# Inverse square roots as one power on POOL, and a column product as a pair of products, in a two-layer hybrid block

## The chip, the cores and the metric

The kernel runs on one core of a Trainium2 chip. The metric is the device time of one execution in microseconds. The names of the engines are those of the profile: PE is the matrix engine (PEld its weight loads), DVE the vector engine, ACT the scalar engine, POOL the GpSimd engine, SP the engine that issues the transfers.

## The reference

Two layers over 1024 latent and 256 context tokens of width 1024. Each layer normalises and modulates its input, projects it once, and runs three mixers side by side: a state space scan in two directions, grouped-query attention, and differential attention. Their outputs are concatenated and projected. What matters here are the places where a root mean square is inverted:

```python
def rmsnorm(x, g):
    xf = x.astype(jnp.float32)
    y = xf * lax.rsqrt(jnp.mean(xf * xf, axis=-1, keepdims=True) + EPS)
    return y.astype(x.dtype) * g
...
        # scan: one root per token
        return rmsnorm(y * jax.nn.silu(z.astype(y.dtype)), norm_g).astype(z.dtype)
...
        # grouped-query attention: one root per token and head, 4 query and 2 key heads
        q = rmsnorm(p["gq"].reshape(bb, ll, GQA_HEADS, GQA_HEAD_DIM), q_g)
        k = rmsnorm(p["gk"].reshape(bb, ll, GQA_KV_HEADS, GQA_HEAD_DIM), k_g)
...
        # differential attention: two maps, combined, then one root per token and head
        o = attention(q[:, :, 0::2], k[:, :, 0::2], v) - lam * attention(q[:, :, 1::2], k[:, :, 1::2], v)
        o = (rmsnorm(o, norm_g) * (1.0 - lam_init)).astype(v.dtype)
```

The layer's own norms, before the input projection and behind the output projection, are of the same form over 1024 columns.

## The kernel before, in words

Tokens lie in 10 tiles of 128 (two of context, eight latent). A layer runs through stages that overlap at their borders: the split of the input, the projections with the convolution, the scan (a chunk of each direction a step) beside the projections in token rows, the two attentions with the output projection in their gaps, and the layer's end. In the first layer the scan and the token rows lie from about 390 to 640 us of the profile and the attention from there to about 1060; in the second layer the attention lies from about 1620 to 2050.

The program is written engine by engine with few explicit orders: a scheduler takes the instructions with their priorities and fixes each engine's order when the program is built, and each engine then works through its list in that order. So an instruction that waits holds everything behind it on its engine.

The change concerns these helpers, by the names of tiles that the profile shows:

- `rsqrt` makes x to the power -0.5 from the exponent's guess (`nri`, `nrj`: L114, L116) and three Newton steps of three instructions each (`nrt`, `nrt`, `nrr`: L121 to L123), all on DVE: eleven instructions on a tile of 128 rows and 1 to 6 columns.
- `finish` (L732) ends a chunk of the scan: gate, the sum of squares `sa` by ACT, mean and eps on DVE (L741), the root, the product (`yf`, L743) and four transposes on PE.
- `gqa_norm` (L892) normalises the heads of a token tile: ACT squares, DVE sums to `gss` (L899), mean and eps on DVE (L900), the root, the product (`raw`, L902), then the rotation on DVE and POOL.
- `out_b` (L1331) ends an attention head: for the differential kind POOL squares (`osq`), DVE sums to `dss` (L1353), mean and eps on DVE (L1354), the root, and POOL multiplies (`oo`, L1356, and `yk`, L1359).
- `inv_rms` (L221) makes a layer norm's root; its mean and eps (`oms`, L223) read PSUM and stay on DVE.
- `s_pair` (L1279) combines the two maps' exponentials of a row: the first 1024 columns by one DVE instruction (L1292), the last 256 on POOL by a product with a column `cc` (L1296) and a sum (L1297).

POOL's main work in the attention is `pl` (L129), the trailing part of the transposed weights, for which PE's second pass of P V (L1416) waits.

Of the kernel before, what the change touches and what calls it, by code (L numbers as in the profile page):

```python
# [8 lines left out]
F32 = mybir.dt.float32  # L9
# [10 lines left out]
KT = 8            # contraction tiles of the model width  # L20
NT = 10           # token tiles: 0, 1 context, 2..9 latent
# [4 lines left out]
# columns of the per-layer parameter pack  # L26
# [41 lines left out]
def block_kernel(ctx: ExitStack, tc: tile.TileContext, tok, cvec, wmod, pack,  # L68
# [7 lines left out]
    @contextmanager  # L76
    def shifted(by):
        """instructions that the scheduler takes for earlier ones by so many."""
        tc.cur_priority -= by
        yield  # L80
        tc.cur_priority += by
# [13 lines left out]
    pm = []                            # the pack's part that the modulation needs  # L95
# [13 lines left out]

    def rsqrt(x, shape, tag, pl=None):  # L110
        """x -> x**-0.5 elementwise, from the exponent's guess and three Newton steps."""
        pl = pl or small
        yi = pl.tile(shape, I32, name="nri", tag=f"nri{tag}")
        V.tensor_scalar(yi, x.bitcast(I32), 1, None, op0=ALU.logical_shift_right)  # L114
        yj = pl.tile(shape, I32, name="nrj", tag=f"nrj{tag}")
        V.tensor_scalar(yj, yi, -1.0, float(0x5F3759DF), op0=ALU.mult, op1=ALU.add)  # L116
        y = yj.bitcast(F32)
        t = pl.tile(shape, F32, name="nrt", tag=f"nrt{tag}")
        r = pl.tile(shape, F32, name="nrr", tag=f"nrr{tag}")
        for i in range(3):  # L120
            V.tensor_mul(t, y, y)  # L121
            V.scalar_tensor_tensor(t, t, -0.5, x, op0=ALU.mult, op1=ALU.mult)
            V.scalar_tensor_tensor(r, t, 1.5, y, op0=ALU.add, op1=ALU.mult)  # L123
            y = r
        return r

    def lo_part(eng, out_, full, hi):
        """out_ = full - hi, the rest of a value whose leading bits are in hi."""
        eng.tensor_tensor(out_, full, hi.bitcast(F32), op=ALU.subtract)  # L129
# [4 lines left out]
    # silu of the conditioning vectors: [p, k, (lat, ctx)]  # L134
    cth = cp.tile([P, KT, 2], F32, name="cth")
    s2 = cp.tile([P, KT, 32], F32, name="s2")          # a column group of the array wide
# [5 lines left out]
    # modulation of each layer, [p, k, (lat, ctx)]: shift, scale (with the pre-norm gain),  # L142
    # gate (with the post-norm gain)
# [4 lines left out]
    def mod_mm(ps, w, k, g):  # L148
        """a part of the modulation in column group g of the array, its rows 32 g and 32 g + 1."""
        TE.matmul(ps[32 * g:32 * g + 32], s2[:, k], w, start=k == 0, stop=k == KT - 1, tile_position=(0, 32 * g))  # L150

    def modulation(parts, mp, pp, tag):
        """two of (layer, 0: shift, 1: scale, 2: gate), a half of each in a column group of the
        array; a generator of small portions."""
# [34 lines left out]
    rnext = cp.tile([P, NT], F32, name="rnext")     # the next layer's 1 / rms of each token  # L189
    BLK = ((256, 512), (0, 256), (768, 512))        # latent tiles 2..5, context, tiles 6..9  # L190

    def broadcast_row(ps, r, n):
        """r [P tokens, n tiles] as rows on all partitions, [P, n * 128] in PSUM."""
        for j in range(n):
            TE.matmul(ps[:, cs(j)], r[:, j:j + 1].to_broadcast([P, P]), ident, start=True, stop=True)
# [3 lines left out]
    def split_input(name):  # L199
        """leading and trailing part of a layer's input, a tile per column tile."""  # L200
        pl = us.enter_context(pool(name, side="right"))
        return [pl.tile([P, 2, T], F32R, name=f"u{k}") for k in range(KT)]

    def u_tile(l, k, c0, n, hr, x, eng):
        """a tile of the modulated input, split, from the normalised one."""
# [7 lines left out]
    def stats(acc, n, pp, tag, bufs=2):  # L213
        """1 / rms per token from the squares' sums over the column tiles, [P tokens, n / 128]."""
# [11 lines left out]
    def column_squares(pl, ps, x, j):  # L226
        """adds the sums over column tile j's rows of the squares of x to the rows of a column group."""
# [5 lines left out]
    def column_stats(pl, ps, pp, tag):  # L233
        """1 / rms per token of those sums, of which each column group has 32 copies."""
# [14 lines left out]
    def square_sum(pl, acc, x, n, j):  # L249
        """sums of squares over the column tiles, the even and the odd ones."""  # L250
# [8 lines left out]
    u = split_input("u0")  # L259
    def start():  # L260
# [20 lines left out]
        def normalise(bi):  # L281
            """tokens' tiles of a block times 1 / rms, in place."""
# [9 lines left out]
        def mod_tile(q):  # L292
            """scale and shift of two column tiles."""
# [53 lines left out]
    def make_finish(l, ylast, wlast, d_op, hsrc):  # L347
        """the end of a layer: its last block's output, and the next layer's input.  A generator;
        the first portion ends when the next layer's input has its block 0."""
# [51 lines left out]
        def finish():  # L401
            with pool("ow", 2, space=PSUM) as pw, pool("tail", 2) as un:
# [7 lines left out]
                def chain():  # L410
                    """the chain of block 2, in an order of its own before what else there is."""
# [18 lines left out]
    for l in range(DEPTH):  # L430
# [3 lines left out]
        t0 = 2 if last else 0          # first token tile that has an output  # L434
# [13 lines left out]
        d_y = dp.tile([8, NT, P, 2, P], F32R, name=f"y{l}")       # leading and trailing parts  # L448
# [13 lines left out]
        # small per-layer values  # L462
        hw = lt_([P, 48], "hw")      # half of the conv's taps and bias
# [22 lines left out]
        NC1 = 4 if l else 3            # conv tiles that begin with the first blocks  # L486
# [6 lines left out]
        def dt_part(tp):  # L493
# [26 lines left out]
            V.tensor_mul(e_, e_, d_)            # s = e / (2 + e), log1p(e) = 2 atanh(s)  # L520
# [33 lines left out]
        def t_weights(wp, i):  # L554
            """columns tile i of the projection's weights, split."""
# [17 lines left out]
        def t_block(i, bi, w):  # L573
            """columns tile i of the projection, transposed, of a block of tokens."""
# [54 lines left out]
        # the first half; after the first layer block 2 comes later than the others  # L629
# [29 lines left out]
        with pool("wT", 4) as wp, pool("convr", 2) as rw2, pool("conv", 2) as vp:  # L659
# [11 lines left out]
            # the second half; beside it the output projection's weights are split, for later  # L671
# [34 lines left out]
        def state_step(c, dr, xb, S, first):  # L706
            """the state after chunk c (in direction dr) from the one before it."""
# [15 lines left out]
        def y_off(c, dr, bc, S):  # L723
            """what the state before chunk c gives to its outputs."""
# [7 lines left out]
        def finish(c, fp, nb=2):  # L732
            """gate, norm, transpose."""
# [7 lines left out]
            V.tensor_scalar(sa, sa, 1.0 / 512, 4 * EPS, op0=ALU.mult, op1=ALU.add)  # L741
            rr = rsqrt(sa, [P, 1], "s")
# [84 lines left out]
        def qk_split(ck, r, nh, d, nq=0):  # L827
            """r [P, nh * d] -> leading and trailing parts, the first nq heads scaled by DSCALE."""
# [22 lines left out]
        def store_twice(dst, src):  # L851
            """both halves of dst's rows from src [r, 4, 128]."""
# [4 lines left out]
        def dq_out(ck, sf, b0, t):  # L857
            """[qh; qh; ql; ql] of each map."""
# [6 lines left out]
        def dk_out(ck, sf, b0, t):  # L865
            """[kh; kl; kh; kl] of each map."""
# [4 lines left out]
        def gq_out(ck, sf, t, trp):  # L871
            """[qh; qh], [ql; ql]."""
# [4 lines left out]
        def rope(ck, raw, nh, hd, ctab, s_lo, s_hi, full):  # L877
            """raw [P, nh*2*hd] rotated in place by the tables ([P, hd] each, or [P, 2, hd])."""
# [13 lines left out]
        def gqa_norm(ck, raw, parts, t):  # L892
            """per-head norm and rotation of raw [P, heads * 64] in place; parts: (gain, first, heads)."""
# [6 lines left out]
            V.tensor_scalar(ss, ss, 1.0 / 64, EPS, op0=ALU.mult, op1=ALU.add)  # L900
            rr = rsqrt(ss, [P, nh], f"g{nh}")
# [10 lines left out]
        with pool("rot") as rp, pool("tokc", 2) as ck:  # L912
# [7 lines left out]
            gain = {}                                  # q gain with the scores' scale, k gain  # L920
# [4 lines left out]
            # rotary tables with the gains folded in  # L925
# [12 lines left out]
            # chunks: z | dq dk | gq gk gv | dv | gg dg  # L938
# [3 lines left out]
            def tok_chunk(ck, ch, first):  # L942
# [11 lines left out]
                for t in range(first, NT):  # L954
# [9 lines left out]
                    if ch in (0, 4):                   # twice the silu  # L964
# [73 lines left out]
        def load_head(kind, m, ph):  # L1038
            """the transposed leading / trailing parts, doubled, of a head's q and k."""
# [21 lines left out]
        def make_job(kind, m, tq, nq):  # L1061
# [8 lines left out]
            # score pairs: (row, map) twice  # L1070
# [18 lines left out]
        def prefetch(kind, n):  # L1089
            """loads of the head of a kind that comes next in the score rows, after job n."""  # L1090
# [6 lines left out]
        # halves of jobs in order: those of two jobs of different kinds take turns  # L1097
# [25 lines left out]
        # Per job (a head's queries of one block of token tiles): score rows (key axis free) with  # L1123
        # their maximum and exponential, then per key tile a transpose, the split and P V.
        # A differential head's two maps are combined before the transpose.  The score rows run
        # ahead of the key tiles' steps.
# [10 lines left out]
        def out_part(bi, k0, pp, tag, kept=None):  # L1137
            """mix columns k0 .. k0 + 3 of the output projection of a block, added to what is in d_op;
# [487 lines left out]
```

## Time and profile before

| what | value |
|---|---|
| runs | 2101.39 us median of 3 (2097.04 to 2106.61) |
| profiled execution | span 2095.2 us from its first to its last instruction |
| runs above that span | 1.8 to 11.4 us, by the median 6.2 us |
| mean granted TensorE clock | 0.935 |
| instructions | 31014 |

The time of the profiled execution around its span isn't given apart; the runs stand above the span by what the third line says. A busy share is a mean over stages that have different limits.

### The profile page before, as it was taken

The numbers are of one execution on the slowest core, as the hardware profiler recorded it, in microseconds if no ns is written. First come the engines' busy times: TensorE is split into PE (matmuls) and PEld (weight loads), VectorE is DVE, ScalarE is ACT, GpSimd is POOL, SyncE is SP. The second block draws the span as 40 slices with busy tenths as digits, with TensorE's granted clock in tenths as the row PEclk, the third lists the DMA queues.
The fourth block names the chain that finished last, engine by engine and source line by source line (L and its number), as shares of the span: only waits on it lengthen the run. The fifth ranks groups of instructions, "written<-read, shape, count | busy, mean of one in ns | idle before, by whom it ended". The sixth has DMA issues, their size and how long they took to land.

```text
span 2095.2 us, 31014 instructions
## 1 busy us (share of the span) xinstructions
PE 1822.2 (87%) x9936; PEld 1475.8 (70%) x9936; DVE 1565.1 (75%) x4103; ACT 1041.9 (50%) x1955; POOL 1162.7 (55%) x1007
## 2 busy tenths in 40 slices
PE   5899999898979999888988797998798898989885
PEld 4587777777767668777765486877777776768773
DVE  5777567777759878799858477577687787888974
ACT  4444233334347766676634354233333676767651
POOL 4535355654227657668735335556543577877741
PEclk9899999899989999999989898998998999999997
DMA  9157557856795988586665148668656956457455
GB/s 289 44 197 235 174 178 205 265 176 203 213 267 167 283 257 261 165 248 201 216 218 186 33 151 283 207 188 247 218 157 208 278 172 180 140 157 212 145 183 184
DMA packets 360003, 418.61 MB, mean 200 GB/s; under 512 B 38752, under 2 KB 252832, under 8 KB 359840
## 3 DMA queue, kind: packets, MB, share of 16 engines
q1 hardware_dynamic: 359840, 416.64, 64.0%
q8 instruction: 78, 1.28, 0.2%
q14 instruction: 85, 0.70, 0.1%
HBM read 282.18 MB, written 134.38 MB: 199 GB/s over the span
## 4 chain that ended last, share of the span: by engine, by line
PE 38%; DVE 26%; DMA 16%; POOL 6%; issue 6%; ACT 4%; SPq 3%; DVEq 0%; POOLq 0%; ACTq 0%
DVE pt L1244 6%; PE sc L1242 4%; DMA ab<-acs 3%; PE tp L1373 3%; PE prj L962 3%; PE prj L961 3%; PE prj L963 3%; PE ops L343 2%; PE ops L344 2%; PE ops L345 2%; PE po L1416 2%; PE po L1415 2%; DMA op<-o 2%; DMA q<-dq 2%; DMA wof<-in_wout_dram 2%
## 5 line engine op out<-in xcount | busy, mean ns | idle before, releaser
L129 POOL TENSOR_TENSOR pl<-pf,ph 128x512 fp32r<-128x512 f32 x283 | 374.2, 1327 | 197.2 <-DVE ph L1395 80.4
L1244 DVE TENSOR_SCALAR_CACHE_REDUCE pt<-sc 128x512 f32<-128x512 f32 (+1 forms) x600 | 335.3, 587 | 71.6 <-PE sc L1242 62.8
L1257 ACT ACTIVATE pt<-pt,nm 128x1280 f32<-128x1280 f32 x192 | 262.4, 1366 | 132.1 <-DVE nm L1255 130.1
L961 PE MATMUL prj<-wh,u 128*128 128x512 f32 (+1 forms) x768 | 298.8, 391 | 27.1 <-DVE th L967 13.7
L962 PE MATMUL prj<-wl,u 128*128 128x512 f32 (+1 forms) x768 | 295.9, 386 | 8.0 <-POOL wl L129 5.3
L963 PE MATMUL prj<-wh,u 128*128 128x512 f32 (+1 forms) x768 | 293.9, 384 | 0.0
L1373 PE MATMUL tp<-ident,pt 128*128 128x128 f32 x1312 | 209.5, 283 | 4.9 <-ACT pf L1383 3.5
L1416 PE MATMUL po<-pl,vt 128*128 128x256 f32 x644 | 184.4, 308 | 18.6 <-POOL pl L129 14.9
L1415 PE MATMUL po<-ph,vt 128*128 128x256 f32 x644 | 187.7, 304 | 14.5 <-ACT ot L1420 6.3
L1383 ACT COPY pf<-tp 128x512 f32<-128x512 f32 x289 | 166.6, 580 | 66.3 <-PE tp L1373 30.9
L961 PEld LDWEIGHTS prj<-wh,u 128*128 128x128 f32 x768 | 153.1, 200 | 54.3 <-DVE th L967 15.6
L1373 PEld LDWEIGHTS tp<-ident,pt 128*128 128x128 f32 x1312 | 160.4, 145 | 29.5 <-ACT pf L1383 8.2
L962 PEld LDWEIGHTS prj<-wl,u 128*128 128x128 f32 x768 | 153.6, 200 | 33.5 <-POOL wl L129 6.6
L1242 PE MATMUL sc<-dk,q 128*128 128x512 f32 (+1 forms) x400 | 148.2, 416 | 31.2 <-DVE pt L1244 21.3
L963 PEld LDWEIGHTS prj<-wh,u 128*128 128x128 f32 x768 | 153.6, 200 | 23.2
L1416 PEld LDWEIGHTS po<-pl,vt 128*128 128x128 f32 x644 | 126.8, 197 | 39.4 <-POOL pl L129 27.4
L1415 PEld LDWEIGHTS po<-ph,vt 128*128 128x128 f32 x644 | 127.1, 197 | 29.5 <-ACT ot L1420 9.5
L607 DVE SCALAR_TENSOR_TENSOR cacc<-craw,hw,cacc 128x1284 f32<-128x1284 f32 (+1 forms) x64 | 118.5, 1853 | 33.4 <-ACT cacc L604 21.9
L582 PE MATMUL prj<-u,wTh 128*128 128x512 f32 x256 | 108.4, 423 | 23.4 <-DVE u L210 17.0
L343 PE MATMUL ops<-y,wo 128*128 128x512 f32 (+1 forms) x304 | 119.0, 391 | 7.4 <-DMA y<-y 6.8
L1296 POOL TENSOR_SCALAR pt<-pt,cc 128x256 f32<-128x256 f32 x64 | 103.1, 1612 | 38.1 <-DVE cc L1288 16.1
L1242 PE MATMUL sc<-gk,q 128*128 128x256 f32 (+1 forms) x400 | 111.7, 384 | 14.1 <-DVE pt L1244 11.8
(287 smaller groups left out, 4448.1 us busy)
## 6 DMA issues: line engine op xcount, KB each, us to landing
wo<-wo SPq DMA_DIRECT2D x80, 512.0 KB, 4.8
wm<-in_wmod_dram SPq DMA_DIRECT2D x48, 512.0 KB, 5.9
dk<-dk SPq DMA_DIRECT2D x16, 1280.0 KB, 7.9
ab<-acs SPq DMA_DIRECT2D x18, 1024.0 KB, 7.6
wo<-wos SPq DMA_DIRECT2D x32, 512.0 KB, 3.6
wf<-in_wtok_dram SPq DMA_DIRECT2D x64, 256.0 KB, 4.0
y<-y SPq DMA_DIRECT2D x30, 512.0 KB, 5.5
op<-o SPq DMA_DIRECT2D x48, 256.0 KB, 4.4
```

The lines of the kernel that those rows point to most:

```text
L129: eng.tensor_tensor(out_, full, hi.bitcast(F32), op=ALU.subtract)
L343: TE.matmul(o, wa[:, k], y[:, :, 0], start=first, stop=False)
L961: TE.matmul(ps[:, c0:], uh, wh[k][:, c0:], start=k == 0, stop=False)
L962: TE.matmul(ps[:, c0:], uh, wl[k][:, c0:], start=False, stop=False)
L963: TE.matmul(ps[:, c0:], ul, wh[k][:, c0:], start=False, stop=k == KT - 1)
L1242: TE.matmul(ps[:, 0:b - a].rearrange("p (t c) -> p t c", c=P), q[:, jb.q0 + j], kt[:, a // P:b // P], start=x == 0, stop=x == len(qq) - 1)
L1244: V.tensor_scalar(ts[r][:, a:b], ps[:, 0:b - a], -1.0, None, op0=ALU.mult, op1=ALU.min, accum_out=mts[r][:, i:i + 1])
L1257: S_.activation(e, e, AF.Exp, bias=nm, scale=-1.0, accum_out=jb.s2[:, j, mp_:mp_ + 1])
L1373: TE.transpose(tp[:, j * P:(j + 1) * P], jb.pt[2 * hf + j % 2][:, cs(2 * s + j // 2)], ident)
L1383: S_.copy(pf[:, :w_], tp[:, :w_])
L1415: TE.matmul(o, vv, a[:, c], start=k == 0, stop=False)
L1416: TE.matmul(o, vv, b[:, c], start=False, stop=k == jb.nk - 1)
```

## The change

Each root becomes one instruction on POOL, a power with the tile `mhalf` of -0.5. For `finish`, `gqa_norm` and `out_b` the mean and eps go to POOL too (`inv_root`, tile `irm`). In `s_pair` the product with the column becomes a pair of products, the second with 1.0. The rest of the diff removes comments, so that line numbers move by one to four.

```diff
+    mhalf = cp.tile([P, 8], F32, name="mhalf")
+    G.memset(mhalf, -0.5)
+
     def rsqrt(x, shape, tag, pl=None):
         pl = pl or small
-        yi = pl.tile(shape, I32, name="nri", tag=f"nri{tag}")
-        V.tensor_scalar(yi, x.bitcast(I32), 1, None, op0=ALU.logical_shift_right)
-        yj = pl.tile(shape, I32, name="nrj", tag=f"nrj{tag}")
-        V.tensor_scalar(yj, yi, -1.0, float(0x5F3759DF), op0=ALU.mult, op1=ALU.add)
-        y = yj.bitcast(F32)
-        t = pl.tile(shape, F32, name="nrt", tag=f"nrt{tag}")
         r = pl.tile(shape, F32, name="nrr", tag=f"nrr{tag}")
-        for i in range(3):
-            V.tensor_mul(t, y, y)
-            V.scalar_tensor_tensor(t, t, -0.5, x, op0=ALU.mult, op1=ALU.mult)
-            V.scalar_tensor_tensor(r, t, 1.5, y, op0=ALU.add, op1=ALU.mult)
-            y = r
+        G.tensor_tensor(r, x, mhalf[:, 0:shape[1]], op=ALU.pow)
         return r
 
+    def inv_root(total, shape, mean, eps, tag):
+        m = small.tile(shape, F32, name="irm", tag=f"irm{tag}")
+        G.tensor_scalar(m, total, mean, eps, op0=ALU.mult, op1=ALU.add)
+        return rsqrt(m, shape, tag)
...
         def finish(c, fp, nb=2):
-            V.tensor_scalar(sa, sa, 1.0 / 512, 4 * EPS, op0=ALU.mult, op1=ALU.add)
-            rr = rsqrt(sa, [P, 1], "s")
+            rr = inv_root(sa, [P, 1], 1.0 / 512, 4 * EPS, "s")
...
         def gqa_norm(ck, raw, parts, t):
-            V.tensor_scalar(ss, ss, 1.0 / 64, EPS, op0=ALU.mult, op1=ALU.add)
-            rr = rsqrt(ss, [P, nh], f"g{nh}")
+            rr = inv_root(ss, [P, nh], 1.0 / 64, EPS, f"g{nh}")
...
             def s_pair(jb, pair):
-                        G.tensor_scalar(b, b, c[:, 1:2], None, op0=ALU.mult)
+                        G.tensor_scalar(b, b, c[:, 1:2], 1.0, op0=ALU.mult, op1=ALU.mult)
...
             def out_b(jb):
-                    V.tensor_scalar(ss[:, :nq], ss[:, :nq], 1.0 / 64, EPS, op0=ALU.mult, op1=ALU.add)
-                    rr = rsqrt(ss[:, :nq], [P, nq], f"a{nq}")
+                    rr = inv_root(ss[:, :nq], [P, nq], 1.0 / 64, EPS, f"a{nq}")
```

The program has 69 roots: 18 in `finish` (one column), 20 in `gqa_norm` (18 of six columns, 2 of two), 20 in `out_b` (16 of four, 4 of two) and 11 in `inv_rms` (four or two). All but those of `inv_rms` move their mean and eps too, 58 instructions. The order of every engine is made anew by the scheduler, so that it differs in many places. Two of them matter here.

On DVE, in `gqa_norm` of the first layer's fourth token tile, the order before is this, from the sum of squares to the first product of the second Newton step (a second and third step of the same three instructions follow, and then `raw<-raw,nrr`):

```order
L899 TENSOR_REDUCE gss<-gsq 128x6
L900 TENSOR_SCALAR gss<-gss 128x6
L114 TENSOR_SCALAR nri<-gss 128x6
L116 TENSOR_SCALAR nrj<-nri 128x6
L121 TENSOR_TENSOR nrt<-nrj 128x6
L122 SCALAR_TENSOR_TENSOR nrt<-nrt,gss 128x6
L123 SCALAR_TENSOR_TENSOR nrr<-nrt,nrj 128x6
L121 TENSOR_TENSOR nrt<-nrr 128x6
```

And this is DVE's order at the same place of the changed kernel:

```order
L897 TENSOR_REDUCE gss<-gsq 128x6
L899 TENSOR_TENSOR raw<-raw,nrr 128x384
L879 TENSOR_TENSOR t_4253<-raw,Sqg 128x4x32
L881 TENSOR_TENSOR t_4253<-raw,Sqg 128x4x32
L879 TENSOR_TENSOR t_4258<-raw,Skg 128x2x32
```

The product that needs the root now stands right behind the sum, with nothing of DVE's between the two.

POOL's order at that tile before is this:

```order
L890 TENSOR_TENSOR raw<-raw,t_4270 128x256
L129 TENSOR_TENSOR vs<-raw,vs 128x2x64
L890 TENSOR_TENSOR raw<-raw,t_4275 128x128
L129 TENSOR_TENSOR st<-raw,st 128x6x64
L129 TENSOR_TENSOR vs<-raw,vs 128x2x64
```

In the changed kernel it is this:

```order
L123 TENSOR_SCALAR irm<-gss 128x6
L117 TENSOR_TENSOR nrr<-irm,mhalf 128x6
L128 TENSOR_TENSOR st<-raw,st 128x6x64
L128 TENSOR_TENSOR vs<-raw,vs 128x2x64
L888 TENSOR_TENSOR raw<-raw,t_4253 128x256
```

The mean and the power stand ahead of the split `st` of the tile before and of this tile's `vs`, so both now wait for DVE's sum.

In the attention, on POOL, this is the first layer's head of four blocks before, from the square's neighbour to the head's end:

```order
L1347 TENSOR_TENSOR yk<-oo,gg 128x2x64
L129 TENSOR_TENSOR pl<-pf,ph 128x512
L1296 TENSOR_SCALAR pt<-pt,cc 128x256
L1297 TENSOR_TENSOR pt<-pt 128x256
L129 TENSOR_TENSOR pl<-pf,ph 128x512 x2
L1356 TENSOR_TENSOR oo<-oo,nrr 128x256
L1359 TENSOR_TENSOR yk<-oo,gg 128x4x64
```

And this is the changed kernel at that head:

```order
L128 TENSOR_TENSOR pl<-pf,ph 128x512
L123 TENSOR_SCALAR irm<-dss 128x4
L1293 TENSOR_SCALAR pt<-pt,cc 128x256
L117 TENSOR_TENSOR nrr<-irm,mhalf 128x4
L1344 TENSOR_TENSOR yk<-oo,gg 128x2x64
L1294 TENSOR_TENSOR pt<-pt 128x256
L128 TENSOR_TENSOR pl<-pf,ph 128x512
L1352 TENSOR_TENSOR oo<-oo,nrr 128x256
```

The head's mean and power now stand among POOL's other work, ahead of a `pl` for which PE waits; the product of the maps' columns moved in between them.

## Rows read from the trace of the kernel before

**Rows 1.** The page: busy time of each engine, and the last chain's shares.
```profile
PE 1822.2 (87%) x9936; PEld 1475.8 (70%) x9936; DVE 1565.1 (75%) x4103; ACT 1041.9 (50%) x1955; POOL 1162.7 (55%) x1007
PE 38%; DVE 26%; DMA 16%; POOL 6%; issue 6%; ACT 4%; SPq 3%; DVEq 0%; POOLq 0%; ACTq 0%
```

**Rows 2.** Windows: length, busy PE, PEld, DVE, ACT, POOL, granted clock, DMA share.
```profile
700.00:850.00 150.00, 144.30 (x919) 109.05 (x918) 119.30 (x392) 101.16 (x194) 97.49 (x93) 1.00 0.86 265
850.00:1000.00 150.00, 127.72 (x762) 107.82 (x760) 133.60 (x423) 99.26 (x174) 110.90 (x96) 0.92 0.67 205
...
1480.00:1600.00 120.00, 101.50 (x512) 84.50 (x511) 97.35 (x337) 45.27 (x110) 56.67 (x58) 0.90 0.60 182
...
1700.00:1850.00 150.00, 132.26 (x801) 109.00 (x800) 125.90 (x409) 107.31 (x184) 115.30 (x95) 0.99 0.57 169
```

**Rows 3.** Whole-span sums of L114, L116, L121, L122, L123, L741, L900, L1354.
```profile
sum 2096.00, DVE 24.30; mean DVE 2.21
sum 2096.00, DVE 18.28; mean DVE 1.66
sum 2096.00, DVE 54.84; mean DVE 4.99
sum 2096.00, DVE 53.73; mean DVE 4.88
sum 2096.00, DVE 59.48; mean DVE 5.41
sum 2096.00, DVE 2.67; mean DVE 0.24
sum 2096.00, DVE 12.77; mean DVE 1.16
sum 2096.00, DVE 9.13; mean DVE 0.83
```

**Rows 4.** Timeline around 650 us, a head's end on DVE and POOL: start, length.
```profile
650.27 1.29 POOL L129 TENSOR_TENSOR pl<-pf,ph 128x512 fp32r<-128x512 f32 x1
650.37 1.21 DVE L123 SCALAR_TENSOR_TENSOR nrr<-nrt,nrj 128x2 f32<-128x2 f32 x1
...
652.59 0.16 DVE L123 SCALAR_TENSOR_TENSOR nrr<-nrt,nrr 128x2 f32<-128x2 f32 x1
...
652.83 0.40 POOL L1356 TENSOR_TENSOR oo<-oo,nrr 128x128 f32<-128x128 f32 x1 [1.27 <-DVE nrr L123]
```

**Rows 5.** The chain that ended last, one undisturbed root's first and last pieces.
```profile
1167.18 0.18 DVE nri L114
...
1169.15 0.17 DVE nrr L123
```

**Rows 6.** The same chain: first and last of 265 pieces of L114 to L123.
```profile
49.99 1.00 DVE nri L114
...
2075.91 0.17 DVE nrr L123
```

**Rows 7.** POOL's groups and lines: mean ns, or ns min/median/max.
```profile
L592 POOL MEMSET craw<- 128x2 f32 x32 | 2.5, 98 | 17.3 <-PE pt L509 10.6 <-DVE cacc L611 5.3 <-ACT x L207 1.0
L137 POOL MEMSET s<- 128x256 f32 x1 | 0.3, 311 | 0.3 <-POOLq L1615 0.3
...
L129 POOL TENSOR_TENSOR vs<-raw,vs x20: 446/460/898, 459.1 to 1579.5; 128x128 fp32r<-128x128 f32 x20
L129 POOL TENSOR_TENSOR pl<-pf,ph x283: 1260/1287/2275, 605.1 to 2044.2; 128x512 fp32r<-128x512 f32 x142
...
L1296 POOL TENSOR_SCALAR pt<-pt,cc x64: 920/1896/2342, 628.5 to 1981.8; 128x256 f32<-128x256 f32 x64
```

**Rows 8.** The chain again: first and last of five pieces of L1296.
```profile
1737.44 2.17 POOL pt L1296
...
1879.25 0.90 POOL pt L1296
```

## The prediction

> **What bounds the kernel now.** I read the page first: PE is busy for 87% of the span and DVE for 75%, and the chain that ended last runs 38% on PE, 26% on DVE, 16% on DMA and only 6% on POOL [rows 1]. So no engine alone sets the time; what DVE gives back counts only where DVE is last. The windows say where that is. From 700 to 850 us PE is busy for 144 of 150 us at full clock, and nothing that DVE gives back can be worth much there. From 850 to 1000 us DVE is busier than PE, 134 against 128 us, and from 1480 to 1600 us and from 1700 to 1850 us the two are within 7 us of each other [rows 2]. In these stretches a shorter DVE is felt.
>
> Then I asked for the lines that the change removes. The five lines of the root cost DVE 24.3 + 18.3 + 54.8 + 53.7 + 59.5 = 210.6 us, and the three of mean and eps 24.6 us [rows 3]: 235 us, 15% of DVE's busy time, for 817 instructions on at most six columns. Undisturbed, such an instruction takes 0.16 to 0.18 us [rows 4, 5], which for 817 would be some 140 us. The rest, about 95 us, is waiting, and the timeline shows for what: at 650.37 us one of these instructions starts while POOL works on `pl`, lasts 1.21 us where its like takes 0.16, and ends within 0.02 us of POOL's instruction. All the while POOL's own next instruction, `oo`, needs the root, and it stands idle for 1.27 us [rows 4].
>
> How much of this lies on the chain that ended last? Followed piece by piece from one end to the other, it holds 265 pieces of the lines of the root, between the two shown; they are 24 roots of eleven, and their sum is 79.7 us [rows 6]. That is 38% of the 210.6 us, and the same share of mean and eps is 9 us. So 89 us of the chain are work that leaves DVE, 3.7 us a root. A root that nothing disturbs takes 2.1 us from its first piece's start to its last one's end [rows 5].
>
> **The change part by part.**
>
> *DVE loses* 69 roots of eleven instructions and 58 of mean and eps, 235 us. The sums, the products behind them and all else stay. On the chain that is 89 us.
>
> *POOL gains* 58 small instructions for mean and eps and 69 powers. The trace of before has neither on so few columns. For mean and eps, the lower bound is a fill of two columns, 0.098 us, and the upper one a two-input instruction of 128 columns, 0.446 us [rows 7]; I take 0.2. For the power the lower bound is that fill again. For the upper one I ask what eleven separate POOL instructions would take: from 128 to 512 columns two-input instructions rise from 0.46 to 1.287 us at the median [rows 7], which is 2.15 ns a column and about 0.19 us to begin with, so eleven take 2.1 us. A power is one instruction, but of many steps, so that it is nearer to one start than to eleven: I take 0.6 us.
>
> *Two handovers* between DVE and POOL come with a root. In the timeline POOL's `oo` starts 0.08 us after the end of DVE's last step [rows 4]; I take 0.1 each. And a root now queues on POOL, which is busy for 55% of the span, mostly with instructions of 1.29 us [rows 1, 7]: half of one in 55% of the cases is 0.36 us. In `out_b` one handover falls away, since the sum's result goes to POOL and the root is used there; I leave that out, for the queue can be longer there.
>
> So a root costs 0.2 + 0.6 + 0.2 + 0.36 = 1.36 us on the chain in place of 3.7, and 24 of them 33 us in place of 89: 56 us net. With the power at 0.1 us it is 68, with 2.1 us it is 20.
>
> *What waits behind it.* In `gqa_norm` DVE's product by the root now stands directly behind the sum, so DVE idles there for about 1 us (0.2 + 0.6 + 0.2) where it worked for 12 instructions before. It can't be shorter for that than POOL lets it be: the rotation of the tile stands behind, and PE's transposes behind that. In `out_b` a mean that waits for DVE's sum holds the `pl` behind it, and with it PE's second pass of P V; before, `oo` held POOL in the same way for the whole root, as the 1.27 us at 650 us show [rows 4]. That is a shorter wait for a longer one.
>
> *The pair of products.* L1296 takes 0.92 us at its shortest and 1.90 us at the median [rows 7], far above the trend of two-input instructions (0.19 + 256 x 2.15 ns = 0.74 us), though it reads one tile and a column. The long ones begin beside DVE's combination of the same rows. Whether a second product makes it quicker, the trace can't say: the lower bound is a fill of 256 columns, 0.311 us, the upper one no change, 0.92 us. I take 0.5, between the two, which takes 64 x 0.42 = 27 us from POOL, but on the chain it stands only five times [rows 8]: 2 us.
>
> *POOL's load* is then 1163 + 58 x 0.2 + 69 x 0.6 - 27 = 1189 us, 57% of the span, so POOL doesn't become the bound. If the pair brings nothing, it is 58%.
>
> *How much of the 56 us arrives.* Not all of it: behind DVE come PE, with 38% of the chain, and the transfers, with 16% [rows 1], and neither gets shorter. In the window from 700 to 850 us PE is next within 6 us of the whole length, in those after 850 us it is next at 85 to 88% [rows 2]. I take one half, 28 us, since the chain is about as often in stretches of the one kind as of the other; the bounds are nothing and all.
>
> A rule of the Trainium skill speaks against the change: Perfetto Trace Analysis, section Optimizing Scalar/DVE Operations, says that GpSimd and the vector engine share a read port of SBUF, so that moving work between those two might not help. The trace agrees on the sharing, with the 1.21 us at 650.37 us. By that rule the net would be about nothing, the third case below. I weigh it less, because eleven chances to wait become two.
>
> **The sum.** 2095.2 - 28 - 2 = 2065 us of span. The runs lie 6.2 us above the profiled span by their median (2101.4 against 2095.2), so 2071 us.
>
> **The rivals.**
>
> - *All of it arrives.* Where DVE is last, its waits on POOL were what kept PE waiting, and PE's order closes up: 56 + 2 us, a time of 2043. For it speak the windows after 850 us, where DVE is as busy as PE or more; against it the PE-bound stretch and the transfers.
> - *Nothing arrives.* DVE's time is given back to waits: DVE stands at `raw<-raw,nrr` while POOL is in another instruction, POOL's two new instructions meet DVE's two-input ones, and PE and the transfers set the pace. Only the pair's 2 us remain: 2099. For it speaks the wait at 650.37 us, read the other way round [rows 4].
> - *The power is slow.* POOL takes its list in order, and a routine of several microseconds for a power would sit in front of `pl`, `st` and `raw`. The point from which it decides is where 24 x (p + 0.76) is 89, at p = 2.95 us, above my bound from eleven instructions. With p at 4 us, the chain gets 25 us longer, and POOL gains 276 us of work, where it is already busy for 111 of 150 us from 850 to 1000 us [rows 2]; with as much again for `pl` late there I get 2101 + 25 + 10 = 2136. Against it speaks that POOL's simple instructions cost 0.1 to 0.2 us to start [rows 7]; for it, that L1296 shows a POOL form at well over the trend of its neighbours.
> - *The pair is no quicker.* Then 2 us are lost on the chain: 2073, inside my forecast.
>
> **How the numbers follow.** The likeliest case, some of the gain arriving (2055 to 2090), has 0.43, with 2071 as its time. All or nearly all (below 2055) has 0.20. Nothing (2091 to 2112) has 0.19. The slow power, or a new order that happens to be worse by as much (above 2112), has 0.18. About 0.5%, 10.5 us, is what a measurement of this kernel can tell from no change. So faster by more than that has 0.63, within it 0.19, slower 0.18. The range reaches from 2032, below the case of the full gain, to 2116, into the slow case.
>
> **What the profile of the changed kernel would show.** Right: DVE's busy time falls from 1565 to about 1330 us; the power takes 0.3 to 1 us for up to six columns; POOL stays under 60%; the chain holds fewer DVE pieces; PE's share rises to 88 or 89%. The half would be wrong if PE's busy share from 850 to 1000 us and after 1700 us stays at 85 to 88% with DVE idle. The price of a power would be wrong if its mean is over 2 us; then DVE's waits for `nrr` would be the longest in the scan. The pair would be wrong if L1296 (then L1293) keeps a shortest time of 0.92 us. The forecast as a whole fails if POOL's new instructions hold `pl` back, which shows as PE's wait at the second pass of P V, or if the new order loses the cover of the transfers in the scan.

## The result, and the profile after

| | before | changed |
|---|---|---|
| runs, median | 2099.81 us (4 runs, 2097.04 to 2106.61) | 2068.65 us (4 runs, 2063.46 to 2074.06) |
| ratio | | 0.9846, 95% interval 0.9825 to 0.9867 |
| span of the profiled execution | 2095.2 us | 2061.6 us |
| mean granted TensorE clock | 0.935 | 0.937 |

The change takes 31 us off the runs; the forecast was 2071 us, 30 below the median shown then. The profiled execution of the changed kernel took 2063.46 us, 1.9 above its span and below its own median, so its span of 33.6 us less shows a little more than the runs. A run of one kernel stands up to 10 us from another, so the medians and intervals decide.

The page of the changed kernel, busy time by engine, which answers to the first line of [rows 1]:

```profile
PE 1806.6 (88%) x9936; PEld 1471.4 (71%) x9936; DVE 1428.5 (69%) x3286; ACT 1041.5 (51%) x1955; POOL 1211.7 (59%) x1135
```

DVE has 817 instructions fewer and 137 us less busy time, POOL 128 more and 49 us more. PE's work is the same in a shorter span. By windows (length, busy PE, PEld, DVE, ACT, POOL, granted clock, DMA share), against [rows 2]:

```profile
700.00:850.00 150.00, 145.07 (x921) 108.87 (x921) 103.92 (x329) 99.48 (x192) 101.24 (x105) 0.99 0.85 265
850.00:1000.00 150.00, 131.37 (x803) 112.82 (x802) 129.59 (x376) 104.08 (x184) 110.15 (x105) 0.94 0.74 227
...
1480.00:1600.00 120.00, 110.23 (x564) 91.00 (x564) 70.43 (x144) 48.18 (x113) 81.14 (x96) 0.93 0.66 201
...
1700.00:1850.00 150.00, 135.28 (x839) 115.47 (x837) 121.63 (x377) 112.79 (x193) 118.05 (x107) 0.98 0.57 167
```

From 700 to 850 us, where PE was busy for 144 of 150 us, nothing could be won, and nothing was. In the other three PE gains 3 to 9 us: where DVE was as busy as PE, PE now gets more done in the same time. From 850 to 1000 us it is busy for 88% instead of 85, from 1700 to 1850 us for 90 instead of 88. The windows don't hold quite the same work in both kernels, since the second layer begins 7 us earlier.

The new instructions on POOL by shape (count, busy us and mean ns, idle before and its releaser), first the powers, then the largest group of mean and eps, then the column's product:

```profile
L117 POOL TENSOR_TENSOR nrr<-irm,mhalf 128x6 f32<-128x6 f32 x18 | 24.9, 1387 | 0.7
L117 POOL TENSOR_TENSOR nrr<-irm,mhalf 128x4 f32<-128x4 f32 x16 | 16.5, 1030 | 0.5
L117 POOL TENSOR_TENSOR nrr<-irm,mhalf 128x1 f32<-128x1 f32 x18 | 10.4, 584 | 0.8
L117 POOL TENSOR_TENSOR nrr<-oms,mhalf 128x4 f32<-128x4 f32 x8 | 8.3, 1038 | 42.5 <-DVE oms L222 42.4
...
L117 POOL TENSOR_TENSOR nrr<-irm,mhalf 128x2 f32<-128x2 f32 x6 | 4.2, 706 | 0.2
L117 POOL TENSOR_TENSOR nrr<-oms,mhalf 128x2 f32<-128x2 f32 x3 | 2.1, 705 | 0.1
...
L123 POOL TENSOR_SCALAR irm<-gss 128x6 f32<-128x6 f32 x18 | 4.7, 261 | 3.5 <-DVE gss L897 2.3
```

The 69 powers take 66.4 us, 0.96 us each, from 0.58 us for one column to 1.39 for six. The column's product, by its line (ns min/median/max), against its row in [rows 7]:

```profile
L1293 POOL TENSOR_SCALAR pt<-pt,cc x64: 474/1089/1820, 630.5 to 1944.1; 128x256 f32<-128x256 f32 x64
```

As a pair it takes 0.474 us at its shortest, where the single product took 0.92.

What became of a single root is best read in the timeline. This is a layer norm's root of the kernel before, as the second layer's input is made, rows of DVE with one of POOL and, last, the weight load of `bps`, PE's product that spreads the root over the rows (start, length, instruction):

```profile
1126.31 0.16 DVE L223 TENSOR_SCALAR oms<-tot 128x4 f32<-128x4 f32 x1 [0.49 <-PE tot L239]
1126.36 1.27 POOL L129 TENSOR_TENSOR wTl<-wTf,wTh 128x512 fp32r<-128x512 f32 x1
...
1126.51 1.15 DVE L114 TENSOR_SCALAR nri<-oms 128x4 int32<-128x4 int32 x1
...
1127.77 0.16 DVE L116 TENSOR_SCALAR nrj<-nri 128x4 int32<-128x4 int32 x1
...
1130.56 1.25 DVE L121 TENSOR_TENSOR nrt<-nrr 128x4 f32<-128x4 f32 x1
...
1133.83 0.16 DVE L123 SCALAR_TENSOR_TENSOR nrr<-nrt,nrr 128x4 f32<-128x4 f32 x1
...
1136.58 1.09 PEld L195 LDWEIGHTS bps<-ident,nrr 128*128 128x128 f32 x8
```

And this is the same root in the changed kernel:

```profile
1122.81 0.15 DVE L222 TENSOR_SCALAR oms<-tot 128x4 f32<-128x4 f32 x1
...
1123.04 1.01 POOL L117 TENSOR_TENSOR nrr<-oms,mhalf 128x4 f32<-128x4 f32 x1 [0.43 <-DVE oms L222]
...
1131.00 0.97 PEld L194 LDWEIGHTS bps<-ident,nrr 128*128 128x128 f32 x8
```

From the mean's start to the root's end it was 7.7 us and is 1.2 us. The undisturbed root of [rows 5] took 2.1 us; here other DVE work stands between the eleven steps, and two of them, of 1.15 and 1.25 us, last until an instruction of POOL ends (the first: 1126.36 + 1.27 us). Over all 69 roots of the kernel before, the time from the first step to the end of the last is 2.1 to 17.3 us, 5.3 at the median; in the changed kernel, from the start of mean and eps to the power's end, it is 0.8 to 4.8 us, 1.7 at the median. The root shown tells of length alone, not of time won: PE takes it up 2.6 us after its end in the kernel before and 7 us after it in the changed one, and the chain that ended last in the kernel before runs over PE's projections there, not over this root.

### The profile page after: what moved, and what is told of

It reads as the page before. It is cut to its first block, busy times and chain, and to the rows that moved or that the text cites. A ratio compares the mean times of both kernels' runs of the same rounds, so it can differ in the third digit from the quotient of the medians.

```text
span 2061.6 us, 30333 instructions
## 1 busy us (share of the span) xinstructions
PE 1806.6 (88%) x9936; PEld 1471.4 (71%) x9936; DVE 1428.5 (69%) x3286; ACT 1041.5 (51%) x1955; POOL 1211.7 (59%) x1135
## 5 line engine op out<-in xcount | busy, mean ns | idle before, releaser
L1412 PEld LDWEIGHTS po<-pl,vt 128*128 128x128 f32 x644 | 126.3, 196 | 33.0 <-POOL pl L128 25.3
L581 PE MATMUL prj<-u,wTh 128*128 128x512 f32 x256 | 109.8, 429 | 22.2 <-DVE u L209 14.2
L582 PE MATMUL prj<-u,wTh 128*128 128x512 f32 x256 | 109.3, 427 | 7.4 <-DVE u L128 6.8
```

Of the source, the lines that this page charges most:

```text
L1412: TE.matmul(o, vv, b[:, c], start=False, stop=k == jb.nk - 1)
```

## The experiments

**My theory**: the gain is the steps of the root, and their waits, leaving DVE; POOL's price is partly covered; the pair is worth little. **The rivals**: the pair did it (A); the scheduler's new order did it by chance (B); POOL no longer waiting for DVE's root did it (C); the gain is the attention's alone (D).

**The pair undone.** In the changed kernel:

```diff
-                        G.tensor_scalar(b, b, c[:, 1:2], 1.0, op0=ALU.mult, op1=ALU.mult)
+                        G.tensor_scalar(b, b, c[:, 1:2], None, op0=ALU.mult)
```

> The changed kernel with the column's product single again, as before; roots by one power on POOL. Theory (the roots leaving DVE bring nearly all of the 31 us; the pair is worth 2 us on the chain): 2066 to 2076, and the line of the product back at a shortest 0.92 us from 0.47. Rival A (the pair matters, since it takes 37 us of POOL's busy time in the attention, where PE waits for POOL's pl): 2082 to 2092. Rival B (the gain is a chance of the new order): anything from 2060 to 2100, since this kernel is ordered anew as well.

2072.74 us, ratio to before 0.986 (0.9833 to 0.9887); the product's shortest is back at 0.919 us. The roots without the pair bring about 28 of the 31 us.

**The pair alone**, the same line the other way round in the kernel before.

> The kernel before with the pair of products alone; roots on DVE. Theory: 2095 to 2101 (2 us or so less, within what can be told). Rival A (the pair matters): 2080 to 2090. Rival B (chance of the order): anything from 2075 to 2115.

2108.45 us, ratio 1.0025 (1.0006 to 1.0045): not faster, if anything slower, and above the range that I gave, though the product's shortest is that of the changed kernel:

```profile
L1296 POOL TENSOR_SCALAR pt<-pt,cc x64: 470/1446/1822, 631.9 to 1993.9; 128x256 f32<-128x256 f32 x64
```

Rival A falls. The pair does what it says on POOL, and it brings nothing that can be told from what a new order is worth.

**The guess without Newton steps**, on DVE, which leaves out the refinement of all the roots:

```diff
-        for i in range(3):
-            V.tensor_mul(t, y, y)
-            V.scalar_tensor_tensor(t, t, -0.5, x, op0=ALU.mult, op1=ALU.mult)
-            V.scalar_tensor_tensor(r, t, 1.5, y, op0=ALU.add, op1=ALU.mult)
-            y = r
-        return r
+        return y
```

> The kernel before with the three Newton steps left out on DVE (the exponent's guess alone, so the roots are about 3% off): 621 small DVE instructions fewer, nothing added on POOL. Theory (DVE's own work and its waits are what the change removes, and POOL gives part of it back): at least as fast as the changed kernel, 2050 to 2070. Rival C (it is not the work on DVE but that POOL no longer waits for DVE's root, so a shorter root on DVE brings little): 2085 to 2100. Rival B (chance of the order): anything.

2068.59 us, ratio 0.985 (0.9823 to 0.9878): the time of the changed kernel, with nothing of it on POOL. So what counts is that nine of eleven dependent steps leave DVE's list; that the rest runs on POOL is not what brings the time. Rival C, a shorter root on DVE that brings little, falls. The run doesn't keep POOL's wait as it was, though: `oo` stood less before the root, from the first row to the second (us in total, times, longest; kernel before, then this run):

```profile
POOL oo L1356 <- DVE nrr L123: 14.6, 9, 2.4
...
POOL oo L1351 <- DVE nrj L116: 5.2, 8, 1.4
```

These 9 us are less than a third of the gain, and no run here takes the steps off DVE with POOL's wait left alone. Nor does a run tell the time that the steps take from DVE's other work apart from the time that a root's reader waits.

**The kernel before in another order.**

```diff
-LEAD = 30
+LEAD = 31
```

> The kernel before with one number of the schedule changed (the score rows' lead over the key tiles, LEAD, 31 for 30), which makes another order of the same instructions. Theory: within 10 us of before, 2090 to 2110. Rival B (an order made anew is worth as much as the change): more than 20 us off, either way.

2107.63 us, ratio 1.004 (1.0021 to 1.0058). This other order of the same instructions is worth 7 to 8 us. That is also what the pair alone showed, so that one can't be told from its new order.

**The changed kernel in another order**, by the same line.

> The changed kernel in another order, by the same number of the schedule (LEAD 31 for 30). Theory (the gain is work and waits that leave DVE, whatever the order): 2060 to 2082, as the changed kernel (2069) give or take the 8 us that another order was worth for the kernel before. Rival B (chance of the order): back above 2090.

2070.4 us, ratio 0.9869 (0.9849 to 0.9888). In the one order the change brings 31 us, in the other 2107.6 - 2070.4 = 37. Rival B falls as an account of the whole gain, as far as two orders can say; differences below 10 us in a single order can be the order's.

**The scan's roots alone**: `finish` and `gqa_norm` as in the change, the rest as before. In this run and the next ones the changed kernel's `rsqrt` on POOL is called `rsqrt_p` where both are needed.

```diff
-            V.tensor_scalar(sa, sa, 1.0 / 512, 4 * EPS, op0=ALU.mult, op1=ALU.add)
-            rr = rsqrt(sa, [P, 1], "s")
+            rr = inv_root(sa, [P, 1], 1.0 / 512, 4 * EPS, "s")
...
-            V.tensor_scalar(ss, ss, 1.0 / 64, EPS, op0=ALU.mult, op1=ALU.add)
-            rr = rsqrt(ss, [P, nh], f"g{nh}")
+            rr = inv_root(ss, [P, nh], 1.0 / 64, EPS, f"g{nh}")
```

> The kernel before with only the roots of finish and gqa_norm (38, in the scan and token rows) by one power on POOL with their mean and eps; the attention's and the layer norms' roots on DVE, the product single. Theory (the gain falls where DVE was last, and the second layer's scan stage gave 27 of the 34 us of span): 2070 to 2085. Rival B (chance of the order): no sum with the next kernel. Rival D (the gain is the attention's): 2095 to 2102.

2099.15 us, ratio 1.0004 (0.9986 to 1.0021): nothing. My expectation was wrong. And in the other order:

> The scan's and the token rows' roots alone on POOL, in another order (LEAD 31). If the nothing that these 38 roots brought was chance of the order, this comes out 10 us or more below the first one (under 2090); if the scan stage gives the time on to later waits in any order, 2092 to 2108.

2107.02 us against 2107.63 for the kernel before in that order: nothing again.

**The attention's and the layer norms' roots alone**: `out_b` and `inv_rms` as in the change.

```diff
-        return rsqrt(ms[:, :n // P], [P, n // P], f"o{n}")
+        return rsqrt_p(ms[:, :n // P], [P, n // P], f"o{n}")
...
-                    V.tensor_scalar(ss[:, :nq], ss[:, :nq], 1.0 / 64, EPS, op0=ALU.mult, op1=ALU.add)
-                    rr = rsqrt(ss[:, :nq], [P, nq], f"a{nq}")
+                    rr = inv_root(ss[:, :nq], [P, nq], 1.0 / 64, EPS, f"a{nq}")
```

> The kernel before with only the roots of out_b (20, attention) and of inv_rms (11, layer norms) by one power on POOL; finish and gqa_norm on DVE, the product single. Theory: 2088 to 2099, the smaller part, and with the kernel of the scan's roots alone the two gains add to 25 to 32 us. Rival D (the gain is the attention's): 2070 to 2080.

2081.1 us, ratio 0.991 (0.9891 to 0.9929): 18 us. That is more than I expected and 1 us short of rival D's range; with the scan's roots alone the two gains add to 18 of 31 us, not to the 25 to 32 that I gave. In the other order:

> The attention's and the layer norms' roots alone on POOL, in another order (LEAD 31). If the 18 us are the roots' own: 2074 to 2090. If chance: over 2092.

2081.37 us, ratio 0.9916 (0.9895 to 0.9937), 26 us below the kernel before in that order. So these 31 roots carry most of the gain in either order, and rival D holds in part. The scan's 38 bring nothing alone, but another 8 us (2081.1 - 2072.7, both with the single product) when the others have moved too; in the other order it is 11 us (2081.4 - 2070.4), the pair included. Both are near what an order is worth.

**The layer norms' roots back on DVE**, all else as in the changed kernel (the line of `inv_rms` above undone).

> The changed kernel with the 11 roots of the layer norms back on DVE (guess and three steps), all else on POOL with the pair. In the changed kernel POOL stands 42 us in front of these powers, in four waits of up to 20.5 us. If that wait holds work that is needed: 2055 to 2064, a version that beats both. If POOL had nothing to do there, as before: 2067 to 2078, for a root then takes 2.2 us on DVE where two of them lie bare on the chain.

2081.12 us, ratio 0.992 (0.9901 to 0.994): 12 us slower than the changed kernel by the medians, 15 by the ratios to the kernel before, worse than either expectation. In this one order eleven roots of 69 are worth over a third of the gain. The timeline of this kernel shows one of them in the second layer's attention, on DVE (first rows and last):

```profile
1948.48 0.15 DVE L239 TENSOR_SCALAR oms<-stt 128x4 f32<-128x4 f32 x1
...
1952.99 0.15 DVE L137 TENSOR_TENSOR nrt<-nrj 128x4 f32<-128x4 f32 x1
...
1953.83 2.16 DVE L1306 SCALAR_TENSOR_TENSOR pt<-pt,cc 128x1024 f32<-128x1024 f32 x1
1955.91 0.68 DVE L138 SCALAR_TENSOR_TENSOR nrt<-nrt,oms 128x4 f32<-128x4 f32 x1
...
1961.34 1.25 DVE L139 SCALAR_TENSOR_TENSOR nrr<-nrt,nrr 128x4 f32<-128x4 f32 x1
...
1966.83 0.15 DVE L139 SCALAR_TENSOR_TENSOR nrr<-nrt,nrr 128x4 f32<-128x4 f32 x1
```

It takes 18.5 us from mean to root; its steps stand apart between the score rows. In the changed kernel the same root is this:

```profile
1935.11 0.14 DVE L222 TENSOR_SCALAR oms<-stt 128x4 f32<-128x4 f32 x1
...
1936.25 1.02 POOL L117 TENSOR_TENSOR nrr<-oms,mhalf 128x4 f32<-128x4 f32 x1
```

2.2 us, though POOL is at a `pl` until 1936.29 us. This root is again an example of length: by the end of the first layer, long before it, this kernel is already 8 us behind the changed one (last `rnext`, the next layer's root, at 1170.6 against 1162.5 us), half of the 16 us at the end. Which of the eleven roots costs the rest isn't shown. The 42.4 us that POOL stands before such powers cost nothing that this run could win back.

**A cheap instruction in the power's place**, in 58 of the 69:

```diff
-        G.tensor_scalar(m, total, mean, eps, op0=ALU.mult, op1=ALU.add)
+        G.tensor_scalar(m, total, 0.0, 1.5, op0=ALU.mult, op1=ALU.add)
...
-        G.tensor_tensor(r, x, mhalf[:, 0:shape[1]], op=ALU.pow)
+        G.tensor_tensor(r, x, mhalf[:, 0:shape[1]], op=ALU.pow if tag[0] == "o" else ALU.add)
```

> The changed kernel with a sum in place of the power in 58 of the 69 roots (all but the layer norms'), so these roots are left out and come out as the number 1; the POOL instructions stand with the same shapes. A sum of that width should take about 0.2 us where the power takes 0.54 to 1.4 us. Theory (a power on the chain costs what it lasts; half of the 38 us of it arrives on some 20 of the 58): 2050 to 2064. Rival E (POOL has slack and the power is covered): 2065 to 2072.

2072.09 us, ratio 0.9869 (0.9841 to 0.9897). The powers of six columns fall from 1387 to 228 ns, POOL's busy time by 47 us, and the time doesn't, though I expected 2050 to 2064 (rival E ends at 2072):

```profile
L117 POOL TENSOR_TENSOR nrr<-irm,mhalf 128x6 f32<-128x6 f32 x18 | 4.1, 228 | 0.7
```

In the scan and in `out_b`, the power's length was covered, or the new order took it back; a difference of some 7 us could hide in that. The granted clock was no lower than the changed kernel's (0.937 to 0.947 against 0.929 to 0.937), so it hides no gain.

**Each power twice.**

```diff
         G.tensor_tensor(r, x, mhalf[:, 0:shape[1]], op=ALU.pow)
+        G.tensor_tensor(r, x, mhalf[:, 0:shape[1]], op=ALU.pow)
```

> The changed kernel with each power issued twice on POOL into the same tile: 69 more powers, some 66 us more POOL work. Theory (about 24 of the roots lie on the chain, a power is 0.96 us by the mean, and half arrives): 10 to 25 us slower than the changed kernel, 2078 to 2094. Rival E (covered by slack on POOL): 2065 to 2073. Rival F (POOL's order holds pl and PE, every power counts): over 2110.

2083.34 us, ratio 0.9921 (0.9898 to 0.9943): 15 us more for 62 us more of POOL's busy time (1212 to 1273), in the expected range. What grew with it is PE's wait for `pl` at its second pass, which in the changed kernel is 25.3 us in total (us in total, times, longest):

```profile
PEld po L1413 <- POOL pl L129: 38.4, 46, 3.5
```

So, in this one order, the present length is near what POOL can hide: less of it brings nothing that shows, as much again costs about a quarter of itself.

**Where the scan's gain went.** The last product of `finish` (`yf` by the root) and the last pair of maps' sums (`cc`) mark the ends of the second layer's scan and of its score rows:

| kernel | last `yf` | last `cc` | span |
|---|---|---|---|
| before | 1619.1 | 1980.4 | 2095.2 |
| scan's roots alone | 1596.5 | 1969.5 | 2093.5 |
| attention's and norms' alone | 1613.2 | 1971.6 | 2077.7 |
| changed | 1584.0 | 1943.6 | 2061.6 |

With the scan's roots alone the last `yf` comes 23 us early, as I had thought; half of that is gone by the end of the score rows and nearly all by the end. In the changed kernel a lead of 35 us is kept. But the mark is not the end of the same work. From the last `rnext`, where the first layer ends, to the last `yf`, the kernel before and the one with the scan's roots alone did this (length, busy PE, PEld, DVE, ACT, POOL, granted clock, DMA share):

```profile
1169.40:1619.10 449.70, 394.75 (x1988) 327.70 (x1989) 324.25 (x721) 174.22 (x356) 227.26 (x193) 0.92 0.62 193
...
1173.40:1596.50 423.10, 367.95 (x1894) 304.60 (x1895) 293.21 (x494) 169.09 (x345) 240.63 (x222) 0.93 0.63 198
```

The stage is 27 us shorter, and PE has been busy for 27 us less in it: 94 of its products have not been run by then and come after the mark, and PE stands idle for 55 us in both. So for PE that lead is work put off, not time won, which fits that it doesn't last. The changed kernel puts off as much there (1895 products by the mark) and gains all the same; why it needs the other roots off DVE for that stays open.

## Why the prediction was right, step by step

The time, 2068.65 for 2071 us, and the direction were right. So was the ground: the root's steps on DVE hold the end, as the run without Newton steps shows by itself, though in one order. That the number came out within 3 us is in part luck: the half was a choice, and several terms were off.

- *DVE's busy time* fell from 1565 to 1428 us, where I said 1330. My 235 us added up lines, but an instruction is counted from its start, and the next can start while it ends: without the 817, DVE's other instructions in the trace of before cover 1381 us, so only 184 us were there to go. The other 48 us came back: what stays on DVE lasts longer now, a little in many places, as the product by the root in `gqa_norm`, whose 18 larger instructions went from 675 to 989 ns by the mean (6 us together).
- *The power* was taken at 0.6 us and measured 0.96, inside the bounds of 0.1 and 2.1; at six columns its 1.39 is above the 1 us that I said the profile would show. Mean and eps at 0.2 were right (0.19 to 0.21 at the median).
- *The pair* was taken at 0.5 and measured 0.474 at the shortest; POOL saved 37 us on it (103 to 66), not 27. That it would bring 2 us is neither shown nor refuted: the changed kernel is 4 us faster with it, the kernel before 5 to 8 us slower, both inside what an order is worth.
- *3.7 us for a root on the chain* was read wrongly. The pieces on the chain are not 24 whole roots: they come from 36 of the 69, 14 of them whole. And they are the root's own instructions alone; what stands between them the chain books on other lines, and from first step to last the 69 roots take 5.3 us at the median and up to 17.3. So the 33 us that POOL gives back were counted on too few roots, and what a root costs its reader was not in the sum at all; whether the two made up for each other no run tells. The changed kernel's chain can be followed back to 1162 us only; over the second layer it holds 55 us less of DVE (273 to 219) and 42 more of POOL (46 to 88), so POOL's price does lie on it.
- *The half that arrives* was a choice and came out at 28 of 56 us by the runs without the pair, but not spread as I had it: I weighed all roots alike, while putting the 11 of the layer norms back costs 12 us in the one order tried and the 38 of the scan bring nothing without the rest.
- *The wait at 650 us* was read as POOL standing idle all the while; its 1.27 us of idle time come after DVE's long instruction, for POOL is at `pl` until 651.56 us.
- *DVE idle behind the sum* was right in its place, but I gave about 1 us a time and it is 2.1. This is the waits' row of the changed kernel, and below it PE's wait for `pl` in the kernel before and in the changed one (us in total, times, longest):

```profile
DVE raw L899 <- POOL nrr L117: 29.7, 14, 4.5
...
PEld po L1416 <- POOL pl L129: 27.4, 43, 2.7
...
PEld po L1412 <- POOL pl L128: 25.3, 39, 2.2
```

30 us of DVE stand there, in place of the steps that were removed; and PE's wait for `pl` at the second pass, which the slow rival needed, did not grow.

- *The rivals*: the slow power falls, with no row of L117 over 1.4 us by the mean and the break-even at 2.95. Nothing arriving falls by the ratio. The full gain, 2043 us, is missed by 25 us. The rule of the Trainium skill that offloading between the two engines might not help (Perfetto Trace Analysis, Optimizing Scalar/DVE Operations) did not decide here. Waits of that look are in both traces: the 1.15 us above, and in the changed kernel a cast of DVE's (`u`, 128x256) that takes 1.36 us at 1125.40 beside a POOL instruction and 0.28 at 1122.88. I argued that fewer instructions are exposed to them; no run here prices that by itself.

## What to carry to other kernels

A chain of small dependent instructions on a busy engine can take several times its undisturbed length from first step to last: look at that time in the timeline, and at whether anything waits for its end, before pricing it. Don't add up busy times of lines whose instructions overlap. One longer instruction on an engine with slack can be better, though each step is dearer there. Where a schedule is made anew with every edit, run a second order of both kernels before believing a difference below 10 us, and don't expect parts of a change to add up. A mark in the trace that comes earlier is a gain only if the same work is done by then.

## What the runs showed of the hardware that was not expected

- A power on POOL takes, by the mean, 0.58 us for one column, 0.71 for two, 1.03 for four and 1.39 for six, about 0.16 us a column above some 0.4 us, by an estimate from these four, where a sum in the same place takes 0.20 to 0.33 us by the mean.
- A product with a column on POOL, 128x256, takes 0.92 us at its shortest as a single product and 0.47 us as a pair of products: the form with more arithmetic is twice as quick.
